# Early FFN blocks of a hybrid decoder layer: gate and up columns made by one product of 512 columns

## The chip, the cores and the metric

One NeuronCore of one Trainium2 chip runs the whole layer in one program. The metric is the device time of one execution in microseconds (us); less is better. Its engines are named as in the profile: PE is TensorE (matmuls), PEld its weight loads, DVE is VectorE, ACT is ScalarE, POOL is GpSimd and SP is SyncE, whose queue issues most DMAs.

## What is computed

A decoder block on x of 256 tokens by 1024 channels, in float32: two token mixers side by side (a gated linear recurrence and an attention), a gated merge, an output projection and a layer norm, then a SwiGLU feed-forward network (FFN) with a second norm. The change touches the FFN's first half:

```python
    mixed = jnp.einsum('bsc,cd->bsd', g_a * z_a + g_b * z_b, w_out)
    x = layer_norm(DN_ALPHA * x + mixed, ln1_w, ln1_b)

    h = jnp.einsum('bsd,df->bsf', x, w_ffn_in)        # (1024, 2 * 2816)
    h_gate, h_up = jnp.split(h, 2, axis=-1)           # columns j and 2816 + j
    y = jnp.einsum('bsf,fd->bsd', jax.nn.silu(h_gate) * h_up, w_ffn_down)
    return layer_norm(DN_ALPHA * x + y, ln2_w, ln2_b)
```

## The kernel before

**Numbers in two parts.** Each operand of a large product is split into a high part in PE's rounded float32 type and a low part that holds the rest. A product is then three matmuls: high by high, low by high and high by low. For weights, `stage` loads a tile of 128 x 2048 floats (1 MB) by one DMA from SP's queue, makes the high part on ACT (`nc.scalar.copy`, L179, called a cast in the profile) and the low part on DVE (L181, a subtraction). The names in the profile are raw, wh and wl.

**Tiles of weights.** `plan` (L71) lists all weight tiles in the order of their use; the host lays each out in that order as one block of `wts` (L749). A tile is some 128-row steps of the contraction (k) by some columns: 8 steps by 256 columns, 4 by 512, or 2 by 1024. The pools hold three raw tiles, four high and four low ones. Tiles marked `held` lie in a pool of their own. `fetch` and `prefetch` call `stage` ahead of use.

**Who sets the order.** The framework gives every engine its own queue, places the semaphores, and orders instructions outside `manual_schedule` by a planner with a timeline of its own. Inside `manual_schedule(engines={PE, DVE, ACT})` the order of these three engines is the order of the program.

**The stage around the change** is such a block written by hand (L654 to L684). Tokens are two halves t of 128. The output projection runs for t = 0, then for t = 1 (`rows_pass`, L566 to L568, tiles wo). The norm of half 0 and its transposes (x1t, L614) fall into the pass of half 1. To cover the norm of half 1, the first features of the FFN are computed early: `EARLY = 4` feature tiles of 128, in four blocks `e[t][i]` of class `FfnEarly`, one for each half t and each pair i of feature tiles. A block multiplies a slice of x1 (stationary, 128 x 128, `x1p[u, k, ts]`, u = 0 high and 1 low) with weight columns (moving, 256 at a time):

```python
e[0][0].gate(); e[0][0].up()
norm1(1)
e[0][0].silu()
e[0][1].gate()
norm1_transpose(1)
prefetch(2)
e[0][1].up(); ...
```

`gate` and `up` are 24 matmuls each (8 steps of k by three), into the two halves of one PSUM bank (2 x 256 floats, fe in the profile). `silu` (L641 on ACT, L642 on DVE) makes silu(gate) times up, named se, and `transpose` (L647, fet) turns it by features and splits it into ah and al for the down projection. The activation and the transposes of the last block, `e[1][1]`, stand behind the block written by hand.

After that, `wide_pair` (L698, L699, tiles fg for gate and fu for up) does the other 18 feature tiles with weights stationary, and `rows_pass` the down projection (tiles wd).

Of the kernel before, what the change touches and what calls it, by code (L numbers as in the profile page):

```python
# [17 lines left out]
P = 128  # L18
# [3 lines left out]
KC = D // P  # L22
H = 8
FF = 2816
NF = FF // P
# [8 lines left out]
EARLY = 4  # L34
HOLD_IN = 2
# [35 lines left out]
def plan():  # L71

    tiles = []

    def add(w, k0, kn, c0, n, held=False):
        tiles.append((w, k0, kn, c0, n, held))

    def feat(w, c0, n):
        for c in range(c0, c0 + n, 256):
            add(w, 0, 8, c, 256)  # L80

    def tok(w, c0, n):
        for c in range(c0, c0 + n, 512):
            add(w, 0, 4, c, 512)
            add(w, 4, 4, c, 512)

    tok("w_in", 1024, 512)
    feat("w_in", 1536, 512)
    feat("w_in", 0, 1024)
    tok("w_in", 2048, 1024)  # L90
    feat("w_in", 3072, 1024)
    feat("w_in", 8192, 1024)
    feat("w_in", 7168, 1024)
    for c in range(2):
        feat("w_in", 5120 + c * 512, 512)
        feat("w_in", 4096 + c * 512, 512)
        tok("w_in", 6144 + c * 512, 512)
    feat("w_branch_a", 0, 1024)
    feat("w_branch_b", 0, 1024)
    for k in range(0, KC, 2):  # L100
        add("w_out", k, 2, 0, 1024)
    for j in range(0, NF, 2):
        add("w_ffn_in", 0, 8, j * P, 256, j < HOLD_IN)
        add("w_ffn_in", 0, 8, FF + j * P, 256, j < HOLD_IN)
    for k in range(0, NF, 2):
        add("w_ffn_down", k, 2, 0, 1024)
    return tiles
# [3 lines left out]
def hybrid_layer_kernel(ctx: ExitStack, tc, x, xT, vecs, wts, ln1_w, ln1_b, ln2_w, ln2_b, consts, out):  # L111
    nc = tc.nc
# [11 lines left out]
    def slot(name, dt=F32):  # L124
        return big.tile([P, 2048], dt, tag="s8", name=name)
# [4 lines left out]
    class Pair:  # L130


        def __init__(self, name):
            self.parts = [slot(f"{name}{i}", F32R).rearrange("p (k u t) -> p k u t", k=KC // 2, u=2)
                          for i in range(2)]
# [13 lines left out]


    loads = plan()
    ready = []
    state = {"next": 0}
# [9 lines left out]
    def stage(pieces=None, eng=nc.vector):  # L163
        i = state["next"]
        if i >= len(loads):
            return
        state["next"] += 1
        _, _, k, _, _, held = loads[i]
        src = wts[i].rearrange("p (k c) -> p k c", k=k)
        view = lambda z: z.rearrange("p (k c) -> p k c", k=k)  # L170
        raw = view(wraw.tile([P, 2048], F32, tag="raw", name=f"raw{i}"))
        if held:
            h, l = view(slot(f"wh{i}", F32R)), view(slot(f"wl{i}", F32R))
        else:
            h = view(whi.tile([P, 2048], F32R, tag="h", name=f"wh{i}"))
            l = view(wlo.tile([P, 2048], F32R, tag="l", name=f"wl{i}"))
        for ks in ks_of(pieces or (k,)):
            nc.sync.dma_start(raw[:, ks, :], src[:, ks, :])
            nc.scalar.copy(h[:, ks, :], raw[:, ks, :])  # L179
            yield  # L180
            eng.tensor_sub(l[:, ks, :], raw[:, ks, :], r32(h[:, ks, :]))  # L181
            yield
        ready.append((h, l))

    def fetch(ahead=LOOKAHEAD):
        while state["next"] < len(loads) and len(ready) < 1 + ahead:
            list(stage())
        return ready.pop(0)

    def prefetch(n):  # L190
        for _ in range(n):
            list(stage())
# [32 lines left out]
    def feat_pair(name, ah=None, al=None):  # L225
        ah, al = (xTh, xTl) if ah is None else (ah, al)
        wh, wl = fetch()
        ps = mm.tile([P, 2, T], F32, tag="mm", name=name)
        for f in range(2):
            feat_steps(ps[:, f, :], wh, wl, f, ah, al, range(KC))  # L230
        return ps
# [43 lines left out]
    with tc.manual_schedule(engines={ET.PE, ET.DVE, ET.Activation}):  # L275
# [10 lines left out]
        for q in range(2):  # L286
            w = stage((1, 1, 1, 1))
# [14 lines left out]
    for j in range(2, 4):  # L302
        ps = feat_pair(f"hf{j}")
# [4 lines left out]
    for j in range(4):  # L308
        ps = feat_pair(f"hq{j}")
# [132 lines left out]
    for j in range(4):  # L442
        ps = feat_pair(f"hg{j}")
# [91 lines left out]
    for j in range(4):  # L535
        side.step()
        ps = feat_pair(f"za{j}", yah, yal)
# [5 lines left out]
    for j in range(4):  # L543
        ps = feat_pair(f"zb{j}", ybh, ybl)
# [12 lines left out]
    def rows_pass(parts, lhs, t, tiles, ktot):  # L557

        ts = slice(t * P, (t + 1) * P)
        lh, ll = lhs  # L560
        for ps, n0 in parts:
            ns = slice(n0, n0 + ps.shape[1])
            for k0, wh, wl in tiles:
                for k in range(2):
                    kk = k0 + k
                    nc.tensor.matmul(ps, lh(kk)[:, ts], wh[:, k, ns], start=(kk == 0), stop=False)  # L566
                    nc.tensor.matmul(ps, lh(kk)[:, ts], wl[:, k, ns], start=False, stop=False)  # L567
                    nc.tensor.matmul(ps, ll(kk)[:, ts], wh[:, k, ns], start=False, stop=(kk == ktot - 1))  # L568
# [32 lines left out]
    x1p = Pair("x1p")  # L601
# [3 lines left out]
    def norm1(t):  # L605
        layer_norm("n1", t, pss[t], xr[:, t, :], wb1, x1[:, t, :])

    def norm1_transpose(t):
        ts = slice(t * P, (t + 1) * P)
        for g in range(2):  # L610
            ps = mm.tile([P, 4, P], F32, tag="mm", name=f"x1t{t}{g}")
            for a in range(4):
                k = 4 * g + a
                nc.tensor.transpose(ps[:, a, :], x1[:, t, k * P:(k + 1) * P], ident)  # L614
            ks = slice(4 * g, 4 * g + 4)
            split(x1p[0, ks, ts], x1p[1, ks, ts], ps)

    class FfnEarly:


        def __init__(self, t, j, wg, wu):
            self.t, self.j, self.wg, self.wu = t, j, wg, wu
            self.ts = slice(t * P, (t + 1) * P)
            self.ps = mm.tile([P, 2, 256], F32, tag="mm", name=f"fe{j}{t}")

        def product(self, i, w):
            (wh, wl), ps, ts = w, self.ps[:, i, :], self.ts
            for k in range(KC):
                nc.tensor.matmul(ps, x1p[0, k, ts], wh[:, k, :], start=(k == 0), stop=False)
                nc.tensor.matmul(ps, x1p[1, k, ts], wh[:, k, :], start=False, stop=False)  # L630
                nc.tensor.matmul(ps, x1p[0, k, ts], wl[:, k, :], start=False, stop=(k == KC - 1))

        def gate(self):
            self.product(0, self.wg)

        def up(self):
            self.product(1, self.wu)

        def silu(self):
            self.sg = sm.tile([P, 256], F32, tag="sg", name=f"se{self.j}{self.t}")  # L640
# [13 lines left out]
    with tc.manual_schedule(engines={ET.PE, ET.DVE, ET.Activation}):  # L654
        tiles = [(2 * q,) + fetch(0) for q in range(4)]
        for q in range(4):
            rows_pass(pss[0], lhs, 0, tiles[q:q + 1], KC)
        prefetch(2)
        norm1(0)
        for q in range(4):  # L660
            if q == 3:
                norm1_transpose(0)
            rows_pass(pss[1], lhs, 1, tiles[q:q + 1], KC)
            if q < 2:
                prefetch(1)
        early = [ready.pop(0) for _ in range(4)]
        e = [[FfnEarly(t, 2 * i, *early[2 * i:2 * i + 2]) for i in range(2)] for t in range(NT)]
        e[0][0].gate()
        e[0][0].up()
        norm1(1)  # L670
        e[0][0].silu()
        e[0][1].gate()
        norm1_transpose(1)
        prefetch(2)
        e[0][1].up()
        e[0][1].silu()
        e[1][0].gate()
        e[1][0].up()
        e[0][0].transpose()
        e[0][1].transpose()  # L680
        e[1][0].silu()
        e[1][1].gate()
        e[1][1].up()
        e[1][0].transpose()  # L684
    e[1][1].silu()
    e[1][1].transpose()
# [18 lines left out]
    for j in range(EARLY, NF, 2):  # L705
        n = j // 2 % 2
# [11 lines left out]
        i, k = divmod(j, KC)  # L718
# [5 lines left out]
    tiles = []  # L724
# [41 lines left out]
```

## Time and profile before

| | |
|---|---|
| median of 3 runs | 513.84 us (513.62 to 514.0) |
| the profiled execution | 513.88 us |
| its span, first to last instruction | 511.8 us |
| PE busy | 501.4 us, 3440 matmuls |
| DVE busy | 338.5 us |
| ACT busy | 249.1 us |
| mean granted clock of PE | 0.998 |

A row of the timeline gives the start in us from the span's start, the duration, engine, line of the kernel, operation, result<-operands by the program's names, the stationary and the moving shape, and a count where rows are merged; in brackets stands the idle time before it and what ended that. A matmul's duration is the time it spends in the pipe; the next one starts before it ends. So the pace of PE is read from starts.

### The profile page before, as it was taken

How to read it: one execution, taken by the hardware profiler on the slowest of the kernel's cores; microseconds unless marked ns; L12 is line 12 of the kernel's file. 1: busy time of each engine (PE TensorE's matmuls, PEld its weight loads, DVE VectorE, ACT ScalarE, POOL GpSimd, SP SyncE). 2: the span in 40 equal slices, each digit the busy share in tenths (PEclk: the TensorE clock that was granted, in tenths of full speed). 3: DMA queues.
4: the chain of work that ended last, by engine and by line, in shares of the span. 5: the costliest groups of instructions: out<-in, count | busy, mean ns of one | idle time of the engine just before them, and what ended most of it. 6: DMA issues, size and time to landing. Idle time of an engine off the chain costs nothing.

```text
span 511.8 us, 8120 instructions
## 1 busy us (share of the span) xinstructions
PE 501.4 (98%) x3440; PEld 467.3 (91%) x3440; DVE 338.5 (66%) x387; ACT 249.1 (49%) x303; POOL 39.9 (8%) x33
## 2 busy tenths in 40 slices
PE   8999999999999999999999999999999999999994
PEld 7899889999999998998999988998888888888884
DVE  5677799997565454776764799555756665643436
ACT  6695354444355445566552553444656556434300
POOL 0000000000020063352010000000000000000000
PEclk9999999999999999999999999999999999999999
DMA  7978544343424445543567276147555455437002
GB/s 247 374 280 311 184 172 158 106 150 156 165 83 165 167 169 197 198 161 118 227 214 279 104 269 239 48 165 246 166 193 218 165 181 218 178 122 257 32 1 82
DMA packets 15571, 91.70 MB, mean 179 GB/s; under 512 B 1840, under 2 KB 2864, under 8 KB 5552
## 3 DMA queue, kind: packets, MB, share of 16 engines
q1 hardware_dynamic: 14688, 88.04, 47.4%
q0 software_dynamic: 848, 3.15, 1.8%
q8 instruction: 27, 0.44, 0.3%
q14 instruction: 8, 0.07, 0.0%
HBM read 90.13 MB, written 1.05 MB: 178 GB/s over the span
## 4 chain that ended last, share of the span: by engine, by line
PE 94%; DMA 3%; DVE 1%; SPq 1%; ACT 0%; issue 0%; DVEq 0%
PE fg L698 6%; PE fu L698 6%; PE wd L567 4%; PE wd L566 4%; PE wd L568 4%; PE fu L699 3%; PE fg L699 3%; DMA raw<-in_wts_dram 3%; PE sc L363 3%; PE mk L239 2%; PE hq L239 2%; PE hq L238 2%; PE hq L237 2%; PE zb L239 2%; PE za L239 2%; PE mk L238 2%
## 5 line engine op out<-in xcount | busy, mean ns | idle before, releaser
L181 DVE TENSOR_TENSOR wl<-raw,wh 128x2048 fp32r<-128x2048 f32 (+2 forms) x88 | 186.5, 2122 | 121.1 <-ACT wh L179 120.8
L179 ACT CAST wh<-raw 128x2048 fp32r<-128x2048 f32 (+2 forms) x88 | 155.8, 1774 | 147.9 <-PE wd L568 18.4
L698 PE MATMUL fg<-x1p,wh 128*128 128x512 f32 x144 | 50.4, 392 | 0.0
L698 PE MATMUL fu<-x1p,wh 128*128 128x512 f32 x144 | 50.4, 392 | 0.0
L699 PE MATMUL fg<-x1p,wl 128*128 128x256 f32 x144 | 40.3, 280 | 0.0
L699 PE MATMUL fu<-x1p,wl 128*128 128x256 f32 x144 | 40.3, 280 | 0.0
L567 PE MATMUL wd<-wl,ah 128*128 128x512 f32 (+1 forms) x110 | 38.2, 348 | 0.0
L568 PE MATMUL wd<-wh,al 128*128 128x512 f32 (+1 forms) x110 | 38.1, 347 | 0.0
L566 PE MATMUL wd<-wh,ah 128*128 128x512 f32 (+1 forms) x110 | 38.0, 347 | 0.0
L698 PEld LDWEIGHTS fg<-x1p,wh 128*128 128x128 f32 x144 | 26.9, 187 | 5.9
L698 PEld LDWEIGHTS fu<-x1p,wh 128*128 128x128 f32 x144 | 26.9, 187 | 5.9
L699 PEld LDWEIGHTS fg<-x1p,wl 128*128 128x128 f32 x144 | 27.2, 189 | 0.0
L699 PEld LDWEIGHTS fu<-x1p,wl 128*128 128x128 f32 x144 | 27.2, 189 | 0.0
L566 PEld LDWEIGHTS wd<-wh,ah 128*128 128x128 f32 x110 | 20.8, 189 | 2.8
L568 PEld LDWEIGHTS wd<-wh,al 128*128 128x128 f32 x110 | 20.8, 189 | 2.6
L567 PEld LDWEIGHTS wd<-wl,ah 128*128 128x128 f32 x110 | 20.8, 189 | 2.5
L239 PE MATMUL hf<-xTh,wl 128*128 128x256 f32 x64 | 18.6, 291 | 1.4 <-DVE wl L181 1.3
L237 PE MATMUL hf<-xTh,wh 128*128 128x256 f32 x64 | 18.3, 286 | 0.9 <-ACT wh L179 0.9
L239 PE MATMUL za<-yah,wl 128*128 128x256 f32 x64 | 18.5, 288 | 0.0
L238 PE MATMUL za<-yal,wh 128*128 128x256 f32 x64 | 18.4, 288 | 0.0
L237 PE MATMUL hg<-xTh,wh 128*128 128x256 f32 x64 | 18.4, 288 | 0.0
L237 PE MATMUL mk<-xTh,wh 128*128 128x256 f32 x64 | 18.3, 286 | 0.0
(218 smaller groups left out, 1387.5 us busy)
## 6 DMA issues: line engine op xcount, KB each, us to landing
raw<-in_wts_dram SPq DMA_DIRECT2D x78, 1024.0 KB, 4.8
raw<-in_wts_dram SPq DMA_DIRECT2D x8, 256.0 KB, 4.7
xTr<-in_xT_dram SPq DMA_DIRECT2D x8, 128.0 KB, 4.6
raw<-in_wts_dram SPq DMA_DIRECT2D x2, 512.0 KB, 6.4
xr<-in_x_dram POOLq DMA_DIRECT2D x1, 1024.0 KB, 5.4
wb<-in_ln_w_dram POOLq DMA_DIRECT2D x2, 512.0 KB, 6.0
wb<-in_ln_b_dram POOLq DMA_DIRECT2D x2, 512.0 KB, 7.9
out_dram<-y SPq DMA_DIRECT2D x4, 256.0 KB, 2.1
```

What stands on the lines that cost most here:

```text
L179: nc.scalar.copy(h[:, ks, :], raw[:, ks, :])
L181: eng.tensor_sub(l[:, ks, :], raw[:, ks, :], r32(h[:, ks, :]))
L237: nc.tensor.matmul(ps, wh[:, k, wcol], ah[:, kk, :], start=(kk == 0), stop=False)
L238: nc.tensor.matmul(ps, wh[:, k, wcol], al[:, kk, :], start=False, stop=False)
L239: nc.tensor.matmul(ps, wl[:, k, wcol], ah[:, kk, :], start=False, stop=(kk == KC - 1))
L363: nc.tensor.matmul(ps[:, a, :], KL[:, h, :], later(Qt, n, h, 1), start=True, stop=True)
L566: nc.tensor.matmul(ps, lh(kk)[:, ts], wh[:, k, ns], start=(kk == 0), stop=False)
L567: nc.tensor.matmul(ps, lh(kk)[:, ts], wl[:, k, ns], start=False, stop=False)
L568: nc.tensor.matmul(ps, ll(kk)[:, ts], wh[:, k, ns], start=False, stop=(kk == ktot - 1))
L698: nc.tensor.matmul(ps, wh[:, k, wcol], x1p.both(k), start=(k == 0), stop=False)
L699: nc.tensor.matmul(ps[:, 0, :], wl[:, k, wcol], x1p[0, k, slice(0, T)], start=False, stop=(k == KC - 1))
```

## The change

In the first four feature tiles a weight tile holds 4 steps of k by 512 columns, 256 of gate and the 256 of up that belong to them, where it held 8 steps by 256 columns of one of the two. The number of tiles, their size and their order in the stream stay. `FfnEarly.product(q)` takes the q-th of a block's two tiles and makes 12 matmuls of 512 columns into the whole bank; `product(0)` stands where `gate()` stood and `product(1)` where `up()` stood. The later tiles are as before.

```diff
     def add(w, k0, kn, c0, n, held=False):
-        tiles.append((w, k0, kn, c0, n, held))
+        tiles.append((w, k0, kn, c0 if isinstance(c0, tuple) else (c0,), n, held))
...
-    for j in range(0, NF, 2):
-        add("w_ffn_in", 0, 8, j * P, 256, j < HOLD_IN)
-        add("w_ffn_in", 0, 8, FF + j * P, 256, j < HOLD_IN)
+    for j in range(0, EARLY, 2):
+        for k in range(0, KC, 4):
+            add("w_ffn_in", k, 4, (j * P, FF + j * P), 256, j < HOLD_IN)
+    for j in range(EARLY, NF, 2):
+        add("w_ffn_in", 0, 8, j * P, 256)
+        add("w_ffn_in", 0, 8, FF + j * P, 256)
...
     class FfnEarly:
-        def __init__(self, t, j, wg, wu):
-            self.t, self.j, self.wg, self.wu = t, j, wg, wu
+        def __init__(self, t, j, first, second):
+            self.t, self.j, self.w = t, j, (first, second)
             self.ts = slice(t * P, (t + 1) * P)
             self.ps = mm.tile([P, 2, 256], F32, tag="mm", name=f"fe{j}{t}")
 
-        def product(self, i, w):
-            (wh, wl), ps, ts = w, self.ps[:, i, :], self.ts
-            for k in range(KC):
-                nc.tensor.matmul(ps, x1p[0, k, ts], wh[:, k, :], start=(k == 0), stop=False)
-                nc.tensor.matmul(ps, x1p[1, k, ts], wh[:, k, :], start=False, stop=False)
-                nc.tensor.matmul(ps, x1p[0, k, ts], wl[:, k, :], start=False, stop=(k == KC - 1))
-
-        def gate(self):
-            self.product(0, self.wg)
-
-        def up(self):
-            self.product(1, self.wu)
+        def product(self, q):
+            (wh, wl), ps, ts = self.w[q], self.ps, self.ts
+            for k in range(4):
+                kk = 4 * q + k
+                nc.tensor.matmul(ps, x1p[0, kk, ts], wh[:, k, :], start=(kk == 0), stop=False)
+                nc.tensor.matmul(ps, x1p[1, kk, ts], wh[:, k, :], start=False, stop=False)
+                nc.tensor.matmul(ps, x1p[0, kk, ts], wl[:, k, :], start=False, stop=(kk == KC - 1))
...
-        e[0][0].gate()
-        e[0][0].up()
+        e[0][0].product(0)
+        e[0][0].product(1)
         norm1(1)
         e[0][0].silu()
-        e[0][1].gate()
+        e[0][1].product(0)
         norm1_transpose(1)
         prefetch(2)
-        e[0][1].up()
+        e[0][1].product(1)
         e[0][1].silu()
...
     given['wts'] = np.stack([
-        given[w][0][k0 * P:(k0 + kn) * P, c0:c0 + n].reshape(kn, P, n).transpose(1, 0, 2).reshape(P, kn * n)
+        np.concatenate([given[w][0][k0 * P:(k0 + kn) * P, c:c + n] for c in c0], 1)
+        .reshape(kn, P, -1).transpose(1, 0, 2).reshape(P, -1)
         for w, k0, kn, c0, n, _ in plan()])
```

The blocks `e[1][0]` and `e[1][1]` change in the same way.

More of the change, by code (lines that the diff above doesn't have):

```diff
@@ L667, in hybrid_layer_kernel @@
         e = [[FfnEarly(t, 2 * i, *early[2 * i:2 * i + 2]) for i in range(2)] for t in range(NT)]
-        e[0][0].gate()
-        e[0][0].up()
+        e[0][0].product(0)
+        e[0][0].product(1)
         norm1(1)
         e[0][0].silu()
-        e[0][1].gate()
+        e[0][1].product(0)
         norm1_transpose(1)
         prefetch(2)
-        e[0][1].up()
+        e[0][1].product(1)
         e[0][1].silu()
-        e[1][0].gate()
-        e[1][0].up()
+        e[1][0].product(0)
+        e[1][0].product(1)
         e[0][0].transpose()
@@ L681, in hybrid_layer_kernel @@
         e[1][0].silu()
-        e[1][1].gate()
-        e[1][1].up()
+        e[1][1].product(0)
+        e[1][1].product(1)
         e[1][0].transpose()
```

## The prediction

> **What bounds the kernel now.** I read the page first: busy shares, the slices and the chain that ended last.
>
> ```profile
> span 511.8 us, 8120 instructions
> PE 501.4 (98%) x3440; PEld 467.3 (91%) x3440; DVE 338.5 (66%) x387; ACT 249.1 (49%) x303; POOL 39.9 (8%) x33
> PEclk9999999999999999999999999999999999999999
> PE 94%; DMA 3%; DVE 1%; SPq 1%; ACT 0%; issue 0%; DVEq 0%
> ```
>
> TensorE (PE) is busy 98% of the span and carries 94% of the chain, at a granted clock of nine tenths or more in every slice. Any time that a product gives back should therefore come off the end, unless something else was only just in time. Which stage is that? I cut the span into stages with the view of windows (columns: stretch, length, then the busy time of each engine with its count, the clock, the DMA share and GB/s).
>
> ```profile
> 296.30:319.00 22.70, 22.70 (x106) 18.91 (x106) 21.65 (x23) 11.48 (x9) 1.00 (x1) 1.00 0.66 237
> 319.00:343.40 24.40, 24.40 (x206) 24.36 (x205) 13.46 (x19) 9.47 (x11) 1.00 (x1) 1.00 0.33 126
> 343.40:444.00 100.60, 100.60 (x584) 88.74 (x582) 64.93 (x73) 56.43 (x74) 0.00 (x0) 1.00 0.53 189
> 444.00:504.80 60.80, 60.73 (x330) 52.62 (x328) 27.86 (x26) 15.79 (x10) 0.93 (x1) 1.00 0.30 112
> 504.80:511.80 7.00, 0.00 (x0) 0.00 (x0) 3.85 (x8) 0.00 (x0) 0.93 (x1) 0.85 0.20 75
> ```
>
> The change lives in the second row, the early FFN blocks: 24.40 us of 24.40 with PE busy, DVE (VectorE) at 13.46 and ACT (ScalarE) at 9.47. From there to 504.80 PE has no hole worth naming; only a 7.00 us tail of the last norm and store follows. So the early stage is limited by how fast PE takes its matmuls, and so is everything after it up to the tail.
>
> **What the change takes and gives on PE.** A row's duration is the time in the pipe and overlaps the next row; what counts is the step from one start to the next. The rows below, from the timeline (start, duration, engine, line), hold an evenly running stretch of each width: the output projection (wo, 512 columns) and the early blocks (fe, 256 columns).
>
> ```profile
> 297.05 0.40 PE L566 MATMUL wo<-wh,mTh 128*128 128x512 f32 x1
> 315.19 0.39 PE L568 MATMUL wo<-wh,mTl 128*128 128x512 f32 x1
> 316.22 0.48 PE L566 MATMUL wo<-wh,mTh 128*128 128x512 f32 x1
> 316.53 0.40 PE L567 MATMUL wo<-wl,mTh 128*128 128x512 f32 x1
> 319.03 0.28 PE L629 MATMUL fe<-wh,x1p 128*128 128x256 f32 x1
> 327.55 0.28 PE L631 MATMUL fe<-wl,x1p 128*128 128x256 f32 x1
> 327.67 1.04 PE L614 MATMUL x1t<-cst,x 128*128 128x128 f32 x8
> 328.46 0.36 PE L629 MATMUL fe<-wh,x1p 128*128 128x256 f32 x1
> 328.66 0.28 PE L630 MATMUL fe<-wh,x1p 128*128 128x256 f32 x1
> 337.17 0.60 PE L647 MATMUL fet<-cst,se 128*128 128x128 f32 x4
> 337.52 0.36 PE L629 MATMUL fe<-wh,x1p 128*128 128x256 f32 x1
> 343.36 0.38 PE L647 MATMUL fet<-cst,se 128*128 128x128 f32 x2
> ```
>
> *256 columns.* The code issues 72 matmuls (three products of 24) between 319.03 and the transposes of x1: (327.55 − 319.03)/71 = 0.1200 us a step. *512 columns.* From 297.05 to 315.19 lie 80 steps of wo (the 4th to the 84th of its matmuls): 18.14/80 = 0.2268 us. Two steps of 256 cost 0.2400, one of 512 costs 0.2268. Doubling the columns does not double the step, since 0.2268 = a + 512b and 0.1200 = a + 256b give a = 0.0132 us that each matmul pays whatever its width. The wo matmuls are the same instruction that the change makes: an activation's 128x128 slice is loaded and 512 columns of a split weight tile stream past it.
>
> *The sum.* Four blocks (two halves of the tokens, two pairs of feature tiles) of 2 x 24 matmuls are 192, and become 4 x 24 = 96: 192 x 0.1200 − 96 x 0.2268 = 23.04 − 21.77 = 1.27 us. The first matmul after transposes takes longer in both widths: 328.66 − 328.46 = 0.20 against 0.12 and 316.53 − 316.22 = 0.31 against 0.23, so 0.08 each way, which cancels over the joints that stay. Half of the 192 weight loads go too, but they overlap the matmuls, so they are already in the steps and are not counted again. The bounds: if the wider step were like the least favourable short stretch of the rows (316.53 to 319.03, 11 steps of 0.2273), the gain is 1.22. On the other side, starts are read to 0.01 us, which over 71 and 80 steps is 0.04 us in the sum: 1.31 at most. I take the wo stretch of 80 steps, the longest and the nearest.
>
> The Trainium skill ("TensorE: Matmul & The Clock Gate", "Back-to-back issue gap") gives for an isolated warm matmul N/2.4 + 2.5 ns, so a fixed part of 2.5 ns; by it an estimate of the sum would be 96 x 0.0025 = 0.24 us. The trace disagrees, with 13.2 ns from its own two steps. The same section gives 131 ns for sustained matmuls of 512 columns, by which an estimate of the gain would be 23.04 − 12.58 = 10.5 us; the trace's 226.8 ns disagrees with that as well.
>
> **What stays at nothing, and its cover.** Sizes, order and number of the loads, casts and subtractions stay: a tile is still 1024 KB and one 128x2048 cast and subtraction. Only its inside changes, so it holds half of the contraction for gate and up at once, not all of it for one. A block's first product still needs its first tile and the second the other. What shrinks is the time that a product gives to what runs behind it. These are the deadlines (timeline of DVE and ACT):
>
> ```profile
> 322.69 1.41 DVE L585 SCALAR_TENSOR_TENSOR x<-x,n1a,wb 128x512 f32<-128x512 f32 x2
> 326.74 0.42 DVE L642 TENSOR_TENSOR se<-se,fe 128x256 f32<-128x256 f32 x1 [2.64 <-ACT se L641]
> 328.92 1.29 DVE L157 TENSOR_TENSOR x1p<-x1t,x1p 128x512 fp32r<-128x512 f32 x2 [1.76 <-ACT x1p L156]
> 331.21 4.49 DVE L181 TENSOR_TENSOR wl<-raw,wh 128x2048 fp32r<-128x2048 f32 x2 [1.00 <-ACT wh L179]
> 335.62 0.41 DVE L642 TENSOR_TENSOR se<-se,fe 128x256 f32<-128x256 f32 x1
> 338.66 0.41 DVE L642 TENSOR_TENSOR se<-se,fe 128x256 f32<-128x256 f32 x1
> 343.49 1.92 ACT L179 CAST wh<-raw 128x2048 fp32r<-128x2048 f32 x1 [0.98 <-PE fe L630]
> 345.31 0.38 ACT L641 ACTIVATE se<-fe 128x256 f32<-128x256 f32 x1
> 347.64 0.42 DVE L642 TENSOR_TENSOR se<-se,fe 128x256 f32<-128x256 f32 x1
> ```
>
> First, the transposes of x1's second half: PE gets there at 319.03 + 36 x 0.2268 = 327.19 instead of 327.67, and the norm is done at 322.69 + 1.41 = 324.10; 3.1 us remain. Second, the third block needs the split of that half, done at 328.92 + 1.29 = 330.21, or 0.48 earlier since it follows the transposes. PE arrives at 327.19 + 0.79 (transposes) + 0.08 + 12 x 0.2268 = 330.78 instead of 331.42; between 0.6 and 1.1 us remain. Third, and tightest, the second block's gated product. Its multiplication stands on DVE behind two tile subtractions and ends at 335.62 + 0.41 = 336.03, and its transposes come at 330.78 + 24 x 0.2268 = 336.22 instead of 337.17. Even if nothing on DVE moved, 0.19 us would remain; the casts ahead of the subtractions follow the split on ACT, so I expect 0.67. If that cover were gone too, each microsecond that DVE is late would cost one. Fourth, the third block's multiplication ends at 339.07 and is wanted at 336.22 + 0.35 + 0.08 + 5.44 = 342.09. PE thus leaves the last block at 342.09 instead of 343.36: 1.27 us early, the sum again.
>
> **Does it reach the end?** Behind the early stage the tiles' loads wait for subtractions, these for casts, and the casts for weight buffers that PE frees, as in the row of 343.49. They move forward with PE. The chain above names DMA with 3% only, and DVE and ACT use 65% and 56% of 343.40 to 444.00.
>
> The profiled execution took 513.88 us around its span of 511.8 and the median is 513.84, so a microsecond of one is a microsecond of the other: 513.88 − 1.27 = 512.61, and by the median 513.84 − 1.27 = 512.57, so **512.6 us**.
>
> **The rivals.**
>
> *No fixed part to save.* If the early products' 512-column step were 2 x 0.1200 the gain would be zero and the time 513.84. The Trainium skill's fixed part (the page and section above) would put it, as an estimate from that page, at 513.6; the trace's two widths speak against that. For the rival: these blocks accumulate into one bank by turns of three, where nothing of that width ran from x1p in this stage. Against it: wo does the same with its own slices at 0.2268. Chance 0.03.
>
> *The gain is lost behind.* Some tile or buffer after the early stage is ready at a fixed time and not by PE's pace; then a hole of up to 1.27 us opens and the time is 512.9 to 513.84. For it: the order on all engines after the last block is chosen by a planner that sees other costs, and may come out differently. Against it: the row 343.40:444.00 shows PE without a hole, and the first tile that PE wants there after the two prefetched ones is subtracted well ahead of its use:
>
> ```profile
> 342.54 2.29 DVE L181 TENSOR_TENSOR wl<-raw,wh 128x2048 fp32r<-128x2048 f32 x1 [3.46 <-ACT wh L179]
> 349.13 0.39 PE L698 MATMUL fg<-x1p,wh 128*128 128x512 f32 x1
> ```
>
> It is ready at 344.83 and used at 349.13, 4.3 us later, and its cast waits for the last block's first tile, so it moves forward too. Chance 0.08.
>
> *Slower: the last block's transposes come too early in PE's order.* They lie outside the order written by hand. The multiplication that feeds them stands behind a cast on ACT and a subtraction on DVE and ends at 347.64 + 0.42 = 348.06, 4.70 us after PE left the block. The planner put 46 wide matmuls between:
>
> ```profile
> 343.50 0.48 PE L698 MATMUL fg<-x1p,wh 128*128 128x512 f32 x1
> 351.56 0.38 PE L647 MATMUL fet<-cst,se 128*128 128x128 f32 x2
> ```
>
> That leaves 351.56 − 348.06 = 3.50 us. A step of the wide stage is (351.56 − 343.50)/46 = 0.175 us. With fewer than 4.70/0.175 = 27 matmuls between, PE waits; with none it waits 4.70 us and the kernel takes 512.57 + 4.70 = 517.3. It is slower than before by over 0.2% once the wait passes 2.3 us, that is with fewer than about 14 matmuls between. For it: by-hand blocks end in just that pattern, and the block's end moves against everything that the planner times. Against it: the cast, the activation and the multiplication all hang on the block's end and move with it. Chance 0.09.
>
> **How the numbers follow.** The forecast has the remaining 0.80. About 0.2% (1.03 us) is what a measurement of this kernel can tell from no change; the forecast's 1.27 is only a little more. The gain's bounds (1.22 to 1.31), one or two joints of 0.08 us that the planner may add or drop, and the spread of the runs before (513.62 to 514.0, 0.2 either way) put the forecast's own range at 512.1 to 512.9. I give it 0.76 beyond 1.03 us and 0.04 within. With the two rivals that end between, no measurable change has 0.04 + 0.03 + 0.08 = 0.15, and slower 0.09. The range reaches to 513.4, into the lost gain, and stops short of the zero gain and of the slower case; about 0.15 stays outside.
>
> **What would show it.** In the changed profile: 96 matmuls on fe of form 128x512, starting 0.227 us apart; the transposes of x1's second half near 327.2, those of the second block near 336.2 and the last block left near 342.1; no idle time of PE before any of them; PE's busy time down by 1.2 to 1.3 us to about 500.1, PE's loads down by 96. The prediction is wrong if the step of fe is nearer 0.240, if PE waits at the transposes of the second or the last block, or if PE is as early at 342 but not at the last matmul of the down projection (its start before is below).
>
> ```profile
> 504.45 0.28 PE L568 MATMUL wd<-wh,al 128*128 128x256 f32 x1
> ```

## The result, and the profile after

The changed kernel takes 512.38 us (median of 9 runs, 511.97 to 513.76) and the kernel before 513.66 us (median of 9, 513.14 to 514.55). The ratio is 0.9978 with a 95% interval of 0.9969 to 0.9987: 1.28 us faster by the medians, 0.7 to 1.6 us by the interval. The forecast was 512.6 us, by a gain of 1.27 us.

The page after, in the lines that answer to those shown of before (span, engines, clock, chain):

```profile
span 509.9 us, 7928 instructions
PE 500.9 (98%) x3344; PEld 462.9 (91%) x3344; DVE 338.5 (66%) x387; ACT 249.1 (49%) x303; POOL 39.9 (8%) x33
PEclk9999999999999999999999999999999999999999
PE 98%; DMA 1%; DVE 1%; issue 0%; DVEq 0%; ACT 0%; SPq 0%
```

PE has 96 matmuls and 96 weight loads fewer; DVE, ACT and POOL have not changed by a tenth of a microsecond. But the span is 1.9 us shorter, not 1.3, and PE's busy time fell by 0.5 us only, where 1.2 to 1.3 had been named as a sign. The windows say where both come from: the first 60 us, whose end is not the same point of the work in both, and then the stages from the change on (columns as in the prediction):

```profile
0.00:60.00 60.00, 58.03 (x427) 56.38 (x428) 39.80 (x54) 38.63 (x54) 0.20 (x4) 1.00 0.81 282
318.30:341.50 23.20, 23.20 (x110) 19.28 (x109) 13.39 (x19) 9.53 (x12) 1.00 (x1) 1.00 0.33 130
341.50:442.00 100.50, 100.50 (x582) 87.97 (x581) 65.04 (x73) 56.32 (x74) 0.00 (x0) 1.00 0.54 190
```

The same first stretch before, and a wait of PE in it (engine, tile and line, what it waited for: us in total, times, longest) that the trace after does not have:

```profile
0.00:60.00 60.00, 56.64 (x424) 54.37 (x425) 39.06 (x54) 38.00 (x54) 0.20 (x4) 1.00 0.78 281
PE hf L239 <- DVE wl L181: 1.3, 3, 0.8
```

The early stage now starts at 318.31 and not at 319.03. PE was busy for 58.03 of the first 60 us, and for 56.64 before, in code that the change does not touch. The start that is 0.72 us sooner is taken for a difference between two executions and not for an effect: the first four experiments below leave everything ahead of the early stage as it is in the changed kernel, and in their traces it starts at 319.42, 318.58, 319.40 and 319.13, on both sides of the 319.03. The busy time follows from the same rows: 1.4 us more in the first 60, 0.7 less from there to the early stage and 1.2 less in it make the 0.5. The stage itself lasts 23.2 us where it lasted 24.4. Here is its timeline, at the places that the prediction named:

```profile
318.31 0.39 PE L633 MATMUL fe<-wh,x1p 128*128 128x512 f32 x1
326.24 0.39 PE L635 MATMUL fe<-wl,x1p 128*128 128x512 f32 x1
326.47 1.03 PE L617 MATMUL x1t<-cst,x 128*128 128x128 f32 x8
327.26 0.48 PE L633 MATMUL fe<-wh,x1p 128*128 128x512 f32 x1
335.52 0.60 PE L645 MATMUL fet<-cst,se 128*128 128x128 f32 x4
335.88 0.48 PE L633 MATMUL fe<-wh,x1p 128*128 128x512 f32 x1
341.23 0.39 PE L635 MATMUL fe<-wl,x1p 128*128 128x512 f32 x1
341.45 0.39 PE L696 MATMUL fg<-x1p,wh 128*128 128x512 f32 x1
502.55 0.28 PE L571 MATMUL wd<-wh,al 128*128 128x256 f32 x1
```

From the first early matmul to the first instruction behind the last block: 341.45 − 318.31 = 23.14 us, against 343.36 − 319.03 = 24.33, so 1.19 us gained. To the start of the last matmul of the down projection: 502.55 − 318.31 = 184.24 against 504.45 − 319.03 = 185.42, so 1.18. Nothing was given back in the 161 us between.

### The profile page after: what moved, and what is told of

Read it like the earlier page. It is cut to its first block, busy times and chain, and to the rows that moved or that the text cites. A ratio compares the mean times of both kernels' runs of the same rounds, so it can differ in the third digit from the quotient of the medians.

```text
span 509.9 us, 7928 instructions
## 1 busy us (share of the span) xinstructions
PE 500.9 (98%) x3344; PEld 462.9 (91%) x3344; DVE 338.5 (66%) x387; ACT 249.1 (49%) x303; POOL 39.9 (8%) x33
## 4 chain that ended last, share of the span: by engine, by line
PE 98%; DMA 1%; DVE 1%; issue 0%; DVEq 0%; ACT 0%; SPq 0%
PE fu L696 7%; PE fg L696 7%; PE wd L569 4%; PE wd L570 4%; PE wd L571 4%; PE fg L697 3%; PE fu L697 3%; PE sc L366 3%; PE hf L240 2%; PE hf L242 2%; PE hf L241 2%; PE mk L242 2%; PE hq L242 2%; PE hq L241 2%; PE hq L240 2%; PE za L242 2%
## 5 line engine op out<-in xcount | busy, mean ns | idle before, releaser
L241 PE MATMUL hf<-xTl,wh 128*128 128x256 f32 x64 | 18.8, 294 | 0.0
```

The source lines that it names most:

```text
L241: nc.tensor.matmul(ps, wh[:, k, wcol], al[:, kk, :], start=False, stop=False)
```

## The experiments

All times are medians. Ratios, with their 95% intervals, are to the kernel before on the same chip in the same set of runs; its medians in the three sets were 513.66, 513.86 and 513.69 us. The changed kernel was timed in the first set alone, so differences to its 512.38 go from one set to another.

**The width alone.** The weights' tiles of the change stay, the products go back to 256 columns:

```diff
-        def product(self, q):
-            (wh, wl), ps, ts = self.w[q], self.ps, self.ts
-            for k in range(4):
-                kk = 4 * q + k
+        def product(self, i):
+            cs = (slice(0, 256), slice(256, 512))[i]
+            ps, ts = self.ps.rearrange("p i t -> p (i t)")[:, cs], self.ts
+            for kk in range(KC):
+                (wh, wl), k = self.w[kk // 4], kk % 4
...
-                nc.tensor.matmul(ps, x1p[0, kk, ts], wh[:, k, :], start=(kk == 0), stop=False)
+                nc.tensor.matmul(ps, x1p[0, kk, ts], wh[:, k, cs], start=(kk == 0), stop=False)
```

> The changed kernel with its new weight tiles, but each block's product made as 256 gate columns over both tiles and then 256 up columns: 192 matmuls of 256 again. Theory (each matmul pays 0.0132 us whatever its width): steps of 0.120 us, the early stage 1.2 to 1.3 us longer than in the changed kernel, so about 513.6 us, the time of the kernel before. Rival (the gain comes from the tiles' inside or from the order that the planner made after them, not from the width): the time stays near 512.4.

513.58 us, ratio 0.9998 (0.9989 to 1.0007): the whole gain is gone. The window of the early stage is that of the kernel before again, and so is the way that PEld fills it (24.37 of 24.40 us, where the change leaves it free for 4 of 23.2):

```profile
319.40:343.80 24.40, 24.40 (x206) 24.37 (x205) 12.60 (x18) 8.93 (x11) 1.00 (x1) 1.00 0.32 126
```

The same holds up to the last matmul of the down projection: 504.83 − 319.42 = 185.41 us, where the kernel before takes 185.42 and the changed kernel 184.24. So the gain is the width of the products and not the inside of the tiles. The planner's order behind the last block also went back to that of before in this run (the two transposes at 343.75, ahead of the first wide matmul at 343.88), so this run alone does not rule it out; the changed kernel's trace does, since the 1.19 us are there at the end of the block written by hand.

**Is there a fixed part at every width?** The same kernel with the cut at column 384:

```diff
-            cs = (slice(0, 256), slice(256, 512))[i]
+            cs = (slice(0, 384), slice(384, 512))[i]
```

> As e1_two_256, but the 512 columns are cut into 384 and 128: again 192 matmuls. Theory (a step is 0.0132 us plus 0.000417 us a column): 0.173 us for 384 and 0.0665 us for 128, together 0.240, the same as two of 256, so about 513.6 us. Rival (a step has a floor, as the weight load or the start of a matmul needs its time, and the cost at 256 columns is already part of it): steps of 128 at 0.10 us or more, the pace of the eight transposes of x1, so at least 3 us above e1_two_256, near 517.

518.16 us, ratio 1.0085 (1.0069 to 1.0100). My theory failed here and the rival held. The timeline has the two widths side by side:

```profile
319.82 0.33 PE L635 MATMUL fe<-wh,x1p 128*128 128x384 f32 x1
322.59 0.33 PE L636 MATMUL fe<-wl,x1p 128*128 128x384 f32 x1
322.76 0.22 PE L634 MATMUL fe<-wh,x1p 128*128 128x128 f32 x1
322.82 0.27 PE L635 MATMUL fe<-wh,x1p 128*128 128x128 f32 x1
322.94 0.27 PE L636 MATMUL fe<-wl,x1p 128*128 128x128 f32 x1
324.50 0.28 PE L635 MATMUL fe<-wh,x1p 128*128 128x128 f32 x1
322.77 0.19 PEld L635 LDWEIGHTS fe<-wh,x1p 128*128 128x128 f32 x1
322.88 0.19 PEld L636 LDWEIGHTS fe<-wl,x1p 128*128 128x128 f32 x1
322.99 0.19 PEld L634 LDWEIGHTS fe<-wh,x1p 128*128 128x128 f32 x1
```

384 columns: (322.59 − 319.82)/16 = 0.173 us, on the line through 256 and 512 (0.173 was expected). 128 columns: from 322.94 to 324.50 lie 14 steps, 0.111 us each, not 0.0665. Only the first step of 128, up to which the loads had room behind the longer matmuls, takes 0.06 us; from there on the weight loads start 0.11 us apart, and the matmuls with them. So below some width the weight load sets the pace, at 0.111 us (read from these rows; no run changes the load alone), and 96 x (0.111 − 0.0665) = 4.3 us is the difference to the run above (4.6 by the medians). The Trainium skill ("TensorE: Matmul & The Clock Gate", "LDWEIGHTS (loading the stationary operand)") gives a load's time as columns divided by 1.2 in ns, by which an estimate for these 128 is 107 ns. The distance of 111 ns between loads in the trace agrees nearly; a load's own row lasts 0.19 us. At 256 columns the step of 0.120 is only 0.009 us above that pace.

**The place of the last block's transposes.** This was the prediction's slower case. They are put first behind the block on PE, with the order of the first two wide steps fixed after them:

```diff
-    e[1][1].silu()
-    e[1][1].transpose()
...
-    for j in range(EARLY, NF, 2):
+    def wide_step(j):
...
+    with tc.manual_schedule(engines={ET.PE}):
+        e[1][1].silu()
+        e[1][1].transpose()
+        wide_step(EARLY)
+        wide_step(EARLY + 2)
+    for j in range(EARLY + 4, NF, 2):
+        wide_step(j)
```

> The changed kernel, with the last early block's transposes put first behind that block in PE's order, ahead of the two first steps of the wide stage, whose order is fixed on PE too. Nothing else is moved: in the changed kernel's profile the multiplication that feeds these transposes ends at 346.04 and PE leaves the block and the transposes ahead at 341.59. Theory (the place of the transposes is what covers the chain of cast, activation, subtraction and multiplication): PE waits 4.4 us there, near 516.8. Rival (the place does not matter, as the chain moves forward or the time comes back in the wide stage): near 512.4.

520.78 us, ratio 1.0128 (1.0104 to 1.0152): 8.4 us above the changed kernel, where 4.4 were expected. The four runs lie between 518.27 and 521.53, and the one with the trace is the longest. PE's wait, then the windows after the block:

```profile
PE fet L645 <- DVE se L640: 4.2, 1, 4.2
```

```profile
341.50:346.40 4.90, 1.43 (x8) 0.95 (x6) 4.19 (x2) 2.70 (x4) 0.00 (x0) 0.86 0.20 52
346.40:348.00 1.60, 0.82 (x3) 0.82 (x4) 1.06 (x3) 0.10 (x1) 0.00 (x0) 0.50 1.04 435
348.00:350.00 2.00, 2.00 (x7) 1.63 (x6) 0.42 (x1) 0.27 (x1) 0.00 (x0) 0.50 0.96 377
350.00:352.00 2.00, 2.00 (x8) 1.71 (x7) 0.00 (x0) 0.00 (x0) 0.00 (x0) 0.52 0.47 197
352.00:354.00 2.00, 2.00 (x13) 1.77 (x12) 0.42 (x1) 0.37 (x1) 0.00 (x0) 1.00 0.00 0
```

The wait itself is as expected, 4.2 us. But the column behind POOL's, the granted clock, falls to 0.50 during the wait and stays there until about 352: 7 or 8 matmuls in a window of 2 us, where the one behind holds 13 at the full clock. The first wide step shows the price:

```profile
347.52 0.78 PE L694 MATMUL fg<-x1p,wh 128*128 128x512 f32 x1
351.50 0.58 PE L694 MATMUL fg<-x1p,wh 128*128 128x512 f32 x1
351.92 0.28 PE L695 MATMUL fg<-x1p,wl 128*128 128x256 f32 x1
352.04 0.39 PE L694 MATMUL fg<-x1p,wh 128*128 128x512 f32 x1
```

Seven pairs take 352.04 − 347.52 = 4.52 us instead of 7 x 0.347 = 2.43, so 2.1 us more; with the wait that makes 6.3 us. The Trainium skill ("TensorE: Matmul & The Clock Gate", "Part 1: The HAM clock gate") says that an idle window of about 3.4 us halves PE's clock until PE has been busy for such a window. This run agrees: the wait was 4.2 us, and the half clock held to about 352, nearly 5 us after PE resumed at 347.18. The remaining part lies in the wide stage, which ran at the full clock but at a slower pace to its end:

```profile
429.77 0.40 PE L694 MATMUL fg<-x1p,wh 128*128 128x512 f32 x1
431.89 0.40 PE L694 MATMUL fg<-x1p,wh 128*128 128x512 f32 x1
```

Six pairs in 2.12 us are 0.353 a pair, and in the changed kernel six take 2.08 (first and last row below), 0.347 a pair:

```profile
419.93 0.40 PE L696 MATMUL fg<-x1p,wh 128*128 128x512 f32 x1
422.01 0.40 PE L696 MATMUL fg<-x1p,wh 128*128 128x512 f32 x1
```

The wide stage has 288 pairs, so 0.006 x 288 = 1.7 us; 4.2, 2.1 and 1.7 make 8.0. In the two traces the whole loss, from the first early matmul to the last of the down projection, is (512.09 − 319.40) − 184.24 = 8.45 us, about the 8.4 of the medians. Why that pace stays slower is open. The price of the wait was traced in one execution only, and the shortest of the four runs is 3.3 us below it.

**The same rule at another place.** The last 512 columns of the down projection's second half of tokens as one part:

```diff
-row_parts("wd1", [(aux, 512), (aux, 256), (mm, 256)])
+row_parts("wd1", [(aux, 512), (mm, 512)])
```

> The changed kernel, and in the down projection's second half of the tokens the last 512 columns are one part, not two of 256: 66 matmuls of 512 in place of 132 of 256. Theory: PE gains 66 x 0.0132 = 0.87 us; behind the last matmul the residual sum and the statistics run over 512 columns (0.67 and 0.69 us) and not 256 (0.42 and 0.43), 0.5 us more. Net about 0.35 us faster than the changed kernel, near 512.0. Rival (the tail is what matters and the fixed part is hidden there): 0.5 us slower than the changed kernel, near 512.9.

512.02 us, ratio 0.9963 (0.9951 to 0.9976), 0.36 us below the changed kernel by the medians. The intervals of the two ratios overlap, so the times alone do not tell this gain from none; they do speak against the rival's 0.5 us more. The traces show both sides of it. From the first early matmul to the start of the last of the down projection it is 502.24 − 319.13 = 183.11 us, 1.13 less than in the changed kernel, and from there to the end of the span 8.0 us, where the changed kernel takes 7.4: about 0.5 us less in all, where 0.35 was expected. The tail pays for it in DVE (residual sum and statistics behind the last matmul):

```profile
502.24 0.39 PE L571 MATMUL wd<-wh,al 128*128 128x512 f32 x1
502.67 0.69 DVE L577 SCALAR_TENSOR_TENSOR y<-x,wd 128x512 f32<-128x512 f32 x1 [2.34 <-PE wd L571]
503.39 0.69 DVE L578 BATCH_NORM_STATS2 n2s<-y 128x6 f32<-128x512 f32 x1
```

In the changed kernel these two run over 256 columns:

```profile
502.87 0.42 DVE L577 SCALAR_TENSOR_TENSOR y<-x,wd 128x256 f32<-128x256 f32 x1 [1.27 <-PE wd L571]
503.32 0.43 DVE L578 BATCH_NORM_STATS2 n2s<-y 128x6 f32<-128x256 f32 x1
```

**And where a sum has to be bought.** In the features with stationary weights, x high and x low can be moved as one operand of 512 columns, at the price of a copy and a sum for each feature:

```diff
...
-            ps = feat_pair(f"{name}{j}")
+            wh, wl = fetch()
             for f in range(2):
                 c = 2 * j + f
-                nc.scalar.activation(g[:, c, :], ps[:, f, :], AF.Sigmoid, bias=bg[:, b0 + c:b0 + c + 1])
+                ps = mm.tile([P, 2, T], F32, tag="mm", name=f"{name}{j}{f}")
+                wcol = slice(f * P, (f + 1) * P)
+                for k in range(KC):
+                    nc.tensor.matmul(ps, wh[:, k, wcol], xTp.both(k), start=(k == 0), stop=False)
+                    nc.tensor.matmul(ps[:, 0, :], wl[:, k, wcol], xTp[0, k, slice(0, T)],
+                                     start=False, stop=(k == KC - 1))
+                nc.scalar.copy(g[:, c, :], ps[:, 1, :])
+                nc.vector.tensor_add(g[:, c, :], ps[:, 0, :], g[:, c, :])
+                nc.scalar.activation(g[:, c, :], g[:, c, :], AF.Sigmoid, bias=bg[:, b0 + c:b0 + c + 1])
```

> The changed kernel, and the 16 features of the two branch gates are made like the wide FFN stage: high weights times 512 columns (x high and x low side by side), low weights times 256, and the two halves added afterwards by a copy on ACT (0.37 us) and a sum on DVE (0.42 us) for each feature. Theory: 128 pairs of matmuls of 256 become 128 of 512, 128 x 0.0132 = 1.7 us less, near 510.7, if PE waits for none of the sums. Rival (twice the PSUM banks and 0.8 us more behind each feature make PE wait): the gain is eaten, 512.4 or more, at worst 16 x 0.79 = 12.6 us more.

511.28 us, ratio 0.9948 (0.9936 to 0.9961), 1.1 us below the changed kernel by the medians. The stretch of the two gates, first in this run and then in the changed kernel:

```profile
108.30:167.10 58.80, 58.80 (x387) 53.33 (x385) 45.26 (x57) 33.54 (x50) 6.08 (x4) 1.00 0.39 140
```

```profile
108.20:168.50 60.30, 60.30 (x514) 60.30 (x514) 41.38 (x44) 28.79 (x35) 4.02 (x4) 1.00 0.39 137
```

PE is 1.5 us shorter (1.7 expected) and has no hole; DVE and ACT do 4 to 5 us more each beside it, which costs nothing there. Here the intervals of the two ratios lie apart.

**Together.** The two edits above and the features hq and hg in the same manner:

```diff
...
+    def add_up(dst, ps, view=lambda z: z):
+        nc.scalar.copy(dst, view(ps[:, 1, :]))
+        nc.vector.tensor_add(dst, view(ps[:, 0, :]), dst)
...
-        ps = feat_pair(f"hq{j}")
+        for f, ps in wide_feat("hq", j):
...
-        ps = feat_pair(f"hg{j}")
+        for f, ps in wide_feat("hg", j):
```

> The changed kernel with the edits of e4_wd_512 and e5_gates_512, and the 16 features hq and hg made in the same way as the gates: 256 matmuls of 512 in place of 256 pairs' share of 256, so 256 x 0.0133 = 3.4 us and 0.35 us of e4. Theory: near 508.6 if nothing waits, near 509.2 if each group loses as much as the gates did (1.1 of 1.7 us came out). Rival (DVE and ACT, which also carry the recurrence beside hg and the gates, become late): above 510.2, the sum of the two edits alone.

509.41 us, ratio 0.9925 (0.9906 to 0.9943), against 513.69 for the kernel before: 4.3 us faster, and 3.0 below the changed kernel. It is below the rival's 510.2 and near the second sum of the expectation, which was wrong, however: two groups that lose 0.6 us each, as the gates did by the medians, give 509.8 and not 509.2. The time lies between the 508.6 without any loss and this 509.8.

**Too far.** The same for the attention's queries and keys:

```diff
-        ps = feat_pair(f"m{nm}{j}")
+        for f, ps in wide_feat(f"m{nm}", j):
+            add_up(dst[:, 2 * j + f, :], ps)
...
```

> As e6_wd_gates_hgrn_512, and the attention's queries and keys (mq, mk) too: 384 matmuls in all, 384 x 0.0133 = 5.1 us and 0.35 us of e4. Theory: near 507 if nothing waits, 508.5 if each group loses as the gates did. Rival (the rotation now needs the sum first, so one copy and one sum lie between the last matmul and the head's scores, and PE waits): above e6.

510.06 us, ratio 0.9925 (0.9911 to 0.9938): not told apart from the run without it (509.12 to 510.69 against 509.15 to 510.92), though 128 more matmuls of 256 are gone, worth 128 x 0.0133 = 1.7 us. PE now waits far behind the place of the edit:

```profile
PE wo L597 <- DVE mTl L160: 0.6, 2, 0.4
```

```profile
299.13 0.39 PE L596 MATMUL wo<-wl,mTh 128*128 128x512 f32 x1
299.92 0.50 PE L597 MATMUL wo<-wh,mTl 128*128 128x512 f32 x1 [0.40 <-DVE mTl L160]
```

The output projection waits for the low part of its operand. The run before it has no such wait. A wait was expected, but at another place, between the last matmul of the rotation and the scores. The waits are 0.6 us, and their effect is larger, since a matmul that waits starts behind the end of the one ahead and not within it (0.79 us from 299.13 to 299.92, where a step is otherwise 0.227): the output projection lasts from 292.89 to 316.82, 23.93 us, and without the edit from 293.30 to 315.98, 22.68, so 1.25 us are lost there. From the first matmul of the keys to the output projection 1.14 us had been gained (292.89 − 166.96 = 125.93, and 293.30 − 166.23 = 127.07). So the gain is given back in that one stage. DVE makes the awaited part late: it begins its last products ahead of it at 283.73, behind a wait for PE's zb, and at 281.62 without the edit. Why it begins later, with the order on PE and DVE planned anew, is open.

## Why the prediction was right, point by point

*What bounds it.* Right: what PE saved in the early stage stayed saved to the last matmul (1.19 and 1.18 us). The sign that PE's busy time would fall to about 500.1 us did not come (500.9), as PE waited less in the first 60 us of this execution.

*The step.* 512 columns from the slices of x1 take (326.24 − 318.31)/35 = 0.2266 us; 0.2268 was read from the output projection. The kernel with 256 columns and the new tiles has the old time, so the sum's ground is shown and not only argued. What did not hold is "each matmul pays whatever its width": a fixed part of 0.013 us is right at 256, 384 and 512 columns and wrong at 128, where the weight load sets the step. The sum of this change needed only 256 and 512. What the fixed part is stays open: every matmul here has a weight load of its own (3344 of each), so no run tells a cost of the matmul from one of its load.

*The sum.* 1.27 predicted, 1.18 to 1.19 in the trace and 1.28 by the medians. That the medians come within 0.01 us is partly luck, since their interval reaches from 0.7 to 1.6. The 0.08 missing in the trace lie in the stretches behind the transposes, where the prediction let the joints cancel. The 0.08 that the first matmul behind transposes takes longer is itself no cost: eight transposes take 327.26 − 326.47 = 0.79 us and four take 335.88 − 335.52 = 0.36, so one takes 0.108, and the eight end 0.07 sooner than 8 x 0.108. In the third stretch, 335.88 to 341.23, the first step takes 0.31 and the other 22 take (341.23 − 336.19)/22 = 0.229 each:

```profile
336.19 0.40 PE L634 MATMUL fe<-wh,x1p 128*128 128x512 f32 x1
336.43 0.40 PE L635 MATMUL fe<-wl,x1p 128*128 128x512 f32 x1
```

That is 0.05 us over 0.2268. The second stretch, 327.26 to 335.52, is 0.02 us over its 36 steps and the 0.08, and differences of 0.01 us between the rows make the rest.

*The covers.* All held, as sized. Deadlines on DVE after (norm of the second half; split of x1; multiplication of the second block):

```profile
321.96 1.41 DVE L588 SCALAR_TENSOR_TENSOR x<-x,n1a,wb 128x512 f32<-128x512 f32 x2
327.72 1.29 DVE L160 TENSOR_TENSOR x1p<-x1t,x1p 128x512 fp32r<-128x512 f32 x2 [1.60 <-ACT x1p L159]
334.43 0.41 DVE L640 TENSOR_TENSOR se<-se,fe 128x256 f32<-128x256 f32 x1
345.63 0.41 DVE L640 TENSOR_TENSOR se<-se,fe 128x256 f32<-128x256 f32 x1
349.55 0.38 PE L645 MATMUL fet<-cst,se 128*128 128x128 f32 x2
```

The norm ends at 323.37 and the transposes come at 326.47: 3.1 us, as predicted. The split ends at 329.01 and the third block, 12 matmuls behind 327.26, starts at 330.08: 1.07, at the upper end. The tightest, the second block's multiplication, ends at 334.84 and is wanted at 335.52: 0.68, where 0.67 was expected.

*The rivals.* A fixed part that cannot be saved is ruled out by the first experiment, and a gain lost behind by the 1.18 us at the last matmul. The slower case did not come: 349.55 − 346.04 = 3.5 us remain between the last multiplication and its transposes, the same as before. Its mechanism was shown when it was forced, but its price was too low: 517.3 at worst was the wait alone, and 520.8 was measured, since a wait of that length also costs the clock.

## What to carry to other kernels

Read the pace of a matmul from start to start at two widths in the same trace: here 256 columns cost 0.120 us and 512 cost 0.227, so joining two narrow products saves 0.013 us each time, a little that counts on a kernel whose PE hardly stops. At 128 columns the step was 0.111 us, so two points do not give the cost of narrower products. Before joining, list what the shorter product used to cover, in microseconds; a cover that fails costs more than its own length once PE stands long enough to lose its clock (4.2 us of wait cost 6.3 here). Where joining needs a sum afterwards, look where the engine that makes the sum has room: in the gates 1.5 us stayed, and with queries and keys the output projection gave 1.25 us back.

## What was not expected of the hardware

A wait of 4.2 us on PE cost about 6.3 us: the granted clock fell to 0.50 within the wait and stayed there for nearly 5 us after PE resumed. After that the wide stage of the same run stepped at 0.353 us a pair instead of 0.347 for 100 us at a granted clock of 1.00; in the changed kernel nine steps of the early stage after its transposes did the same, (338.28 − 336.19)/9 = 0.232 us instead of 0.227. What switches between the two paces is open.
